# Output pairs of a hybrid decoder layer: sums of y and differences of the weights move from GpSimd to the vector engine, and the slots of the output stage are laid out anew

## The chip, the cores and the metric

The kernel is one program on one core of a Trainium2 chip. The metric is the device time of one execution in microseconds (us), as the median of several runs. The engines are called as the profile calls them: PE (TensorE matmul) with PEld (its weight load), DVE (VectorE), ACT (ScalarE), POOL (GpSimd) and SP (SyncE, which only issues DMAs). Each engine works through its own queue of instructions in order; they wait for one another by semaphores.

## The reference, cut to what matters

One decoder layer over 2048 positions of width 1024, all in float32. Its last step, where most of the change lies, is a product with the output weights, a norm over the row, a gate and a residual:

```python
h = rmsnorm(x, g_pre) * (1.0 + scale[:, None, :]) + shift[:, None, :]
proj = jnp.einsum('bsd,de->bse', h, w_in)
gu, gv, gg, rq, rk, rv, rg = jnp.split(proj, PROJ_SPLITS, axis=-1)
y_gmlp = gmlp_branch(gu, gv, gg, gmlp_ln_g, gmlp_ws, gmlp_bs)
y_ret = retention_branch(rq, rk, rv, rg, positions, ret_gn_g)
y = jnp.concatenate([y_gmlp, y_ret], axis=-1)
y = rmsnorm(jnp.einsum('bsm,md->bsd', y, w_out), g_post)
return x + gate[:, None, :] * y
```

## The kernel before

**Numbers as pairs.** Each float32 operand of the large products is split into a rounded high part (cast on ACT) and a low part (subtracted on DVE), and each product is three matmuls of 128x128 by 128x512: high by high, weights' low part, activations' low part (`mm3`, L255). In `mm3` the third matmul is the one that reads the low part of its first operand, in the output stage the low part `yl` of the y block.

**Stages.** The sequence is worked in two halves of 1024 positions. In each half come the projections by token ("prv", "pqk", "pv"), and then six units (`unit`, kinds r, r, g, u, g, u) in which a block product of 2 by 2 is done with seven products instead of eight (Strassen in Winograd's form: `PRODUCTS`). The seven products need sums of blocks of activations (S1 to S4) and of weights (T1 to T4); their results pass through three banks of PSUM, X, Y and Z, and are added up on DVE. Each unit multiplies its result into y (`used`, L784): on DVE when `ON_V` names the half and the unit, else on POOL.

**The output stage.** After the units of both halves, y is multiplied with the output weights, again by seven products. A pair is two blocks of 128 rows of y; there are eight pairs in groups of `GROUPS_OUT = (2, 1, 1, 1, 1, 1, 1)`. y was written to DRAM when it was finished (`yspill`) and is loaded again as four blocks "ya" a pair (`pair_loads`); `pair_sums` makes S1 to S4 of them ("ys") and splits each operand ("yh", "yl"). The output weights come as raw blocks "or"; `osplit` (L208) forms T1 to T4 and splits them ("wh", "wl"). There are 28 such blocks (seven products by four), and they are kept for the whole stage. `out_tail` (L671) takes the results from the banks "zX", "zY", "zZ" through the partial results s1, u2, u3, g11, c22, c21, c12, squares them on ACT (with "jz" as a dump), and adds x ("xr") before the result is stored.

**The order of the work.** The kernel writes the order out by hand. A slot is one step of a product: three matmuls. `slots.at(d, f)` puts f in the engines' queues d+1 slots later, and in a group of n pairs product i of pair j starts at slot 4*(n*i + j), counted from the group's start. This gives only the order in each queue: an instruction runs as soon as its engine has come to it and its inputs and its space are there. SP's DMAs keep the order in which they are written too.

**Space.** Most tiles take one of 80 slots of 2 KB in the pool `big` (`slot`), each new tile the slot of one that is done. Beside it there is a stack of areas, opened and closed in order: in the second half "ys" (8 tiles; in it lies the first activation block A11 until the last unit's first product is done), then "yT1" (y of the gMLP groups) and "unit1". Where an area is closed and another opened in its place, the tiles of the new one wait for the last users of the old one. In the output stage before, `begin` (L1227) closes all three after the first product and opens "out", from which x and the partial results come.

Of the kernel before, what the change touches and what calls it, by code (L numbers as in the profile page):

```python
# [11 lines left out]
F32 = mybir.dt.float32  # L12
F32R = mybir.dt.float32r
BF16 = mybir.dt.bfloat16
I32 = mybir.dt.int32
AF = mybir.ActivationFunctionType
ALU = mybir.AluOpType
# [4 lines left out]
P = 128  # L22
D = 1024
# [14 lines left out]
EXTRA_PUMPS = {(0, 4): (0, 0, 0, 0, 0, 1, 1), (0, 5): (0, 0, 0, 1, 0, 1, 1), (1, 3): (0, 0, 0, 1, 0, 1, 1),  # L38
               (1, 4): (1, 1, 0, 1, 1, 1, 1), (1, 5): (1, 0, 1, 0, 1, 1, 1)}
SLOTS = 80  # L40
ON_V = ((0, 2), (1, 4), (1, 5))
TOKEN_PASSES = 4
R_WHEN = (0, 2, 5, 6, 8, 9, 10, 11, 12, 14, 15, 16)
UNITS = (("r", 0), ("r", 1), ("g", 0), ("u", 0), ("g", 1), ("u", 1))
GROUP = {"u": 0, "g": 2, "r": 6}
PRODUCTS = (("B11", "A11"), ("T2", "S2"), ("B21", "A12"), ("T3", "S3"), ("T1", "S1"), ("T4", "A22"),
            ("B22", "S4"))
BUILD = {2: ((1, "diag", 0), (8, "row", 0), (12, "diag", 1), (19, "row", 1), (20, "x", 0), (21, "x", 1)),
# [52 lines left out]
def tile_hybrid_layer(ctx: ExitStack, tc, x, xt, wm, wg, win, wun, wout, wst, cols, rows, pos, cst,  # L101
# [40 lines left out]
    def slot(name, shape=(512,), dtype=F32, pool=None):  # L142
        return (pool or big).tile([P, *shape], dtype, name=name, tag="s")
# [9 lines left out]
    def closed(n=1):  # L153
        for _ in range(n):
            areas.pop()
            opens.pop().__exit__(None, None, None)
# [38 lines left out]
    def split(i, r, eng, gap):  # L195
        hi, lo = slot("wh", dtype=F32R), slot("wl", dtype=F32R)
        blocks[i] = (hi, lo)
        S.copy(hi, r)  # L198

        def rest():  # L200
            eng.tensor_tensor(lo, r, hi.bitcast(F32), ALU.subtract)  # L201

        if gap:
            slots.at(gap - 1, rest)
        else:
            rest()

    kept = {}  # L208

    def osplit(i, n, eng, gap):  # L210
        r, (p, kb) = raw.pop(i), divmod(n, 4)
        what = PRODUCTS[p][0]
        if what == "T2":
            t3, t2, t1 = kept["T3", kb], kept["T2", kb], kept["T1", kb] = r["B12"], r["B11"], r["B22"]
            V.tensor_tensor(t3, t1, t3, ALU.subtract)
            V.tensor_tensor(t2, t3, t2, ALU.add)
            slots.at(1, lambda: split(i, t2, eng, gap))
        elif what == "T1":
            t = kept.pop((what, kb))
            G.tensor_tensor(t, t, kept["T2", kb], ALU.subtract)  # L220
            slots.at(3, lambda: split(i, t, eng, gap))
        elif what == "T4":
            t = r["B21"]
            G.tensor_tensor(t, t, kept.pop(("T2", kb)), ALU.subtract)
            slots.at(3, lambda: split(i, t, eng, gap))
        else:
            split(i, kept.pop((what, kb)) if what == "T3" else r[what], eng, gap)

# [377 lines left out]
    ydram = ctx.enter_context(tc.tile_pool(name="ydram", bufs=1, space=bass.MemoryType.DRAM))  # L606
    yd = {}

    def yspill(half, part, cols, queue=SP):
        for q in range(2):  # L610
            if (half, part, q) not in yd:
                yd[half, part, q] = ydram.tile([P, QUAD, 4, P], F32, name=f"yd{half}{part}{q}")
            for n in cols:
                queue.dma_start(yd[half, part, q][:, :, n, :], (yR, yT)[part][half, q][n])


    def pair_loads(half, ch):
        a = {}

        def load():  # L620
            for m in range(2):
                for part in range(2):
                    t = a[f"A{m + 1}{part + 1}"] = slot("ya", (4, P))
                    SP.dma_start(t, yd[half, part, m][:, ch, :, :])

        return a, load

    def pair_sums(a, ops, size, j):

        def op(out, x, y, how):  # L630
            def run():
                if out not in a:
                    a[out] = slot("ys", (4, P))
                G.tensor_tensor(a[out], a[x], a[y], how)  # L634
                if out == "S3":
                    a.pop("A21")
            return run

        def part(key):
            def run():  # L640
                hi, lo = ops[key] = slot("yh", (4, P), F32R), slot("yl", (4, P), F32R)
                src = a[key]
                S.copy(hi, src)  # L643
                slots.at(0, lambda: V.tensor_tensor(lo, src, hi.bitcast(F32), ALU.subtract))  # L644
            return run

        def need(n):
            return 4 * (size * n + j)

        n = [need(i) for i in range(len(PRODUCTS))]  # L650
        return ((n[0] - 8, op("S1", "A21", "A22", ALU.add)), (n[0] - 6, part("A11")),
                (n[1] - 9, op("S2", "S1", "A11", ALU.subtract)), (n[1] - 6, part("S2")),
                (n[3] - 12, op("S3", "A11", "A21", ALU.subtract)), (n[2] - 6, part("A12")),
                (n[3] - 6, part("S3")), (n[6] - 17, op("S4", "A12", "S2", ALU.subtract)),
                (n[4] - 6, part("S1")), (n[5] - 6, part("A22")), (n[6] - 6, part("S4")))
# [15 lines left out]
    def out_tail(half, ch, ops, psum):  # L671
        last = (half, ch) == (1, QUAD - 1)
        ps, tmp, xr = {}, {}, []
        row = [half * HALF + (ch + QUAD * m) * P for m in range(2)]
        ss = small.tile([P, 2, 2], F32, name="zss", bufs=4)
        rs = small.tile([P, 2], F32, name="zrs", bufs=4)
        pools = []

        def temp(name):
            t = tmp[name] = pools[0].tile([P, 512], F32, name=name, tag="k", bufs=10)  # L680
            return t

        def product(n, k):
            a, bank, first = ops[PRODUCTS[n][1]], "XYXYZYZ"[n], n in (0, 1, 4)
            if first and k == 0:
                ps[bank] = psum[0].tile([P, 512], F32, name=f"z{bank}", tag=psum[1])
            mm3(ps[bank], (a[0][:, k, :], a[1][:, k, :]), blocks[OUT_BLOCKS + 4 * n + k],
                first and k == 0, k == 3, not first)

        def square(z, m, n):  # L690
            jk = pools[0].tile([P, 512], BF16, name="jz", tag="j", bufs=2)
            S.activation(jk, z, AF.Square, scale=1.0 / 32.0, accum_out=ss[:, m, n:n + 1])

        def add(dst, bank, other):
            V.tensor_tensor(temp(dst), ps[bank], tmp[other], ALU.add)

        def root(m):
            r = rs[:, m:m + 1]
            G.tensor_scalar(r, ss[:, m, 0:1], ss[:, m, 1:2], EPS, ALU.add, ALU.add)
            G.tensor_tensor(r, r, nhalf[:, 0:1], ALU.pow)  # L700

        def cols(n):
            return slice(n * 512, (n + 1) * 512)

        def gain(dst, z, n):
            V.tensor_tensor(dst, z, gg[:, cols(n)], ALU.mult)

        def result(m, n, zg):
            V.scalar_tensor_tensor(xr[m][:, cols(n)], zg, rs[:, m:m + 1], xr[m][:, cols(n)], ALU.mult,
                                   ALU.add)  # L710
            SP.dma_start(out[row[m]:row[m] + P, cols(n)], xr[m][:, cols(n)])

        def block(name, bank, other, m, n):
            return ((0, lambda: add(name, bank, other)), (1, lambda: square(tmp[name], m, n)),
                    (2, lambda: gain(tmp[name], tmp[name], n)))

        def after(n, begin):
            if n == 0:
                pools.append(begin())
                temp("s1")  # L720
                for m in range(2):
                    xr.append(pools[0].tile([P, D], F32, name="xr", tag="x", bufs=4))
                    SP.dma_start(xr[m], x[row[m]:row[m] + P, :])
            steps = (
                ((0, lambda: S.copy(tmp["s1"], ps["X"])),),
                ((0, lambda: add("u2", "Y", "s1")),),
                ((0, lambda: square(ps["X"], 0, 0)), (1, lambda: gain(temp("g11"), ps["X"], 0))),
                ((0, lambda: add("u3", "Y", "s1")),),
                block("c22", "Z", "u3", 1, 1),
                block("c21", "Y", "s1", 1, 0) + ((3, lambda: root(1)),  # L730
                                                 (8 - 4 * last, lambda: result(1, 0, tmp["c21"])),
                                                 (9 - 4 * last, lambda: result(1, 1, tmp["c22"]))),
                block("c12", "Z", "u2", 0, 1) + ((3, lambda: root(0)),
                                                 (10, lambda: result(0, 0, tmp["g11"])),
                                                 (11, lambda: result(0, 1, tmp["c12"]))))
            for t, fn in steps[n]:
                slots.at(t, fn)

        return product, after
# [481 lines left out]
                prepare(groups[0], len(PRODUCTS) * 4)  # L1221
            unit(half, un, up)

    slots.at(3, partial(yspill, 1, 1, (2, 3), S))
    pools = []

    def begin():  # L1227
        if not pools:
            closed(3)
            pools.append(opened("out"))  # L1230
        return pools[0]

# [2 lines left out]
            prepare(groups[n + 1], len(PRODUCTS) * 4 * len(group))  # L1235
        out_pairs(begin, [g[:3] for g in group])
    slots.flush()
    closed()


# [60 lines left out]
```

## Time and profile before

| what | us |
|---|---|
| median of 3 runs | 889.39 (888.69 to 890.38) |
| the profiled execution | 890.16 |
| its span in the trace | 888.4 |
| PE busy | 849.4 (96% of the span) |
| DVE busy | 670.8 (76%) |
| POOL busy | 386.3 (43%) |
| ACT busy | 311.2 (35%) |

The span runs from the first instruction to the end of the last; the profiled execution's time has 1.8 us beside it. The shares are means over stages that differ: a stage is read from its own rows.

### The profile page before, as it was taken

The page shows a single profiled execution, that of the slowest core. Times are in us where ns is not written, and L with a number is a line of the kernel's source. Part 1 is how long each engine was busy: PE and PEld are TensorE (multiplying, and loading weights), DVE is VectorE, ACT ScalarE, POOL GpSimd, SP SyncE. Part 2 cuts the span into 40 slices and gives each one's busy share as a digit, 9 for nine tenths or more (in the row PEclk, how much of TensorE's full clock was granted, in tenths as well). Part 3 has the DMA queues.
Part 4 walks back from the last instruction along what each step waited for, and adds up shares of the span by engine and source line. Part 5 has one row for each costly group of instructions (what it writes and reads, how often), then busy time and mean ns, then how long its engine had stood idle before and what let it go on. Part 6 is the DMA issues. An engine that isn't in the chain of part 4 may idle for free.

```text
span 888.4 us, 11862 instructions
## 1 busy us (share of the span) xinstructions
PE 849.4 (96%) x4074; PEld 699.1 (79%) x4074; DVE 670.8 (76%) x1255; ACT 311.2 (35%) x611; POOL 386.3 (43%) x423
## 2 busy tenths in 40 slices
PE   2999999999999999999999999999999988999996
PEld 1778888888888788888888888888888766788884
DVE  4989875666994768997786664996369887977775
ACT  4673223232363434421121121364334424333331
POOL 2041354345756446200433333784556163554551
PEclk9999999999999999999999999999999988999999
DMA  8971331210013424744122100012406742465442
GB/s 323 327 259 35 95 108 64 91 36 1 1 60 107 135 63 148 227 141 157 56 84 69 39 1 1 1 48 77 157 17 194 257 165 85 128 229 164 143 150 88
DMA packets 61884, 100.59 MB, mean 113 GB/s; under 512 B 5888, under 2 KB 22400, under 8 KB 61824
## 3 DMA queue, kind: packets, MB, share of 16 engines
q1 hardware_dynamic: 59712, 98.78, 34.0%
q10 hardware_dynamic: 2112, 1.05, 0.4%
q8 instruction: 32, 0.52, 0.2%
q14 instruction: 28, 0.23, 0.1%
HBM read 83.03 MB, written 16.78 MB: 112 GB/s over the span
## 4 chain that ended last, share of the span: by engine, by line
PE 83%; DVE 6%; DMA 4%; issue 3%; ACT 2%; POOL 1%; SPq 0%; ACTq 0%; DVEq 0%; POOLq 0%
PE pqk L258 6%; PE pqk L256 6%; PE pqk L257 6%; PE pY L256 4%; PE pY L258 3%; PE pY L257 3%; PE pv L258 3%; PE pv L256 3%; PE pv L257 3%; PE prv L257 2%; PE prv L256 2%; PE prv L258 2%; PE pX L258 2%; PE pX L257 2%; PE pX L256 2%
## 5 line engine op out<-in xcount | busy, mean ns | idle before, releaser
L256 PE MATMUL pqk<-wh,hh 128*128 128x512 f32 x240 | 102.4, 427 | 0.0
L524 POOL TENSOR_TENSOR rA<-rA,rB 128x512 f32<-128x512 f32 x32 | 42.5, 1328 | 133.1 <-DVE rB L516 99.0
L258 PE MATMUL pqk<-wh,hl 128*128 128x512 f32 x240 | 94.7, 394 | 0.0
L257 PE MATMUL pqk<-wl,hh 128*128 128x512 f32 x240 | 93.9, 391 | 0.0
L538 ACT COPY qkT<-tp 128x512 f32<-128x512 f32 x32 | 18.8, 586 | 160.1 <-PE tp L529 160.1
L201 DVE TENSOR_TENSOR wl<-wr,wh 128x512 fp32r<-128x512 f32 x62 | 64.1, 1047 | 0.2
L258 PEld LDWEIGHTS pqk<-wh,hl 128*128 128x128 f32 x240 | 45.0, 188 | 10.5
L256 PE MATMUL pv<-wh,hh 128*128 128x512 f32 x128 | 52.1, 407 | 0.0
L257 PEld LDWEIGHTS pqk<-wl,hh 128*128 128x128 f32 x240 | 45.4, 189 | 6.8 <-issue 0.2
L256 PEld LDWEIGHTS pqk<-wh,hh 128*128 128x128 f32 x240 | 45.4, 189 | 6.6 <-issue 0.2
L258 PE MATMUL pv<-wh,hl 128*128 128x512 f32 x128 | 50.1, 391 | 0.0
L257 PE MATMUL pv<-wl,hh 128*128 128x512 f32 x128 | 50.0, 390 | 0.0
L634 POOL TENSOR_TENSOR ys<-ya 128x512 f32<-128x512 f32 x16 | 22.3, 1396 | 59.6 <-DMA ya<-yd 37.3
L201 DVE TENSOR_TENSOR wl<-ut,wh 128x512 fp32r<-128x512 f32 x48 | 42.4, 902 | 1.6 <-ACT wh L198 1.4
L514 DVE TENSOR_TENSOR rA<-pqk,cos_t 128x512 f32<-128x512 f32 x28 | 19.2, 687 | 32.0 <-PE pqk L258 32.0
L258 PE MATMUL zY<-wh,yl 128*128 128x512 f32 x96 | 38.7, 404 | 2.7 <-DVE yl L644 2.7
L582 DVE TENSOR_SCALAR yq<-o,gmv,grs 128x128 f32<-128x128 f32 x64 | 23.3, 406 | 23.8 <-POOL grs L575 23.8
L256 PE MATMUL zY<-wh,yh 128*128 128x512 f32 x96 | 38.9, 405 | 2.4 <-ACT yh L643 1.3
L461 ACT ACTIVATE vh<-pv,nbv,rsv 128x128 f32<-128x128 f32 x64 | 24.1, 457 | 47.4 <-POOL nbv L456 47.4
L241 POOL TENSOR_TENSOR ut<-ur,ut 128x512 f32<-128x512 f32 x24 | 36.2, 1508 | 9.8 <-DVE yT L791 7.6
L791 POOL TENSOR_TENSOR yT<-yT,c 128x512 f32<-128x512 f32 x15 | 24.7, 1651 | 35.7 <-DVE c L811 25.9
L198 ACT CAST wh<-ut 128x512 fp32r<-128x512 f32 x48 | 28.7, 620 | 32.7 <-POOL ut L241 32.7
(253 smaller groups left out, 2594.9 us busy)
## 6 DMA issues: line engine op xcount, KB each, us to landing
wr<-in_win SPq DMA_DIRECT2D x64, 256.0 KB, 3.6
ur<-in_wun SPq DMA_DIRECT2D x48, 256.0 KB, 3.6
slab<-in_wm SPq DMA_DIRECT2D x16, 512.0 KB, 6.6
ya<-yd SPq DMA_DIRECT2D x32, 256.0 KB, 5.2
xr<-in_x SPq DMA_DIRECT2D x16, 512.0 KB, 3.8
out<-xr SPq DMA_DIRECT2D x32, 256.0 KB, 2.1
or<-in_wout SPq DMA_DIRECT2D x28, 256.0 KB, 3.5
xt<-in_xt SPq DMA_DIRECT2D x24, 256.0 KB, 4.1
```

The costliest lines, as they stand in the source:

```text
L198: S.copy(hi, r)
L201: eng.tensor_tensor(lo, r, hi.bitcast(F32), ALU.subtract)
L241: G.tensor_tensor(r[name], r[a], r[b], ALU.subtract)
L256: T.matmul(ps, l[0], r[0], start=first, stop=False, skip_group_check=reopened)
L257: T.matmul(ps, l[0], r[1], start=False, stop=False, skip_group_check=reopened)
L258: T.matmul(ps, l[1], r[0], start=False, stop=last, skip_group_check=reopened)
L461: S.activation(vh[:, g, :], ps[:, g * P:(g + 1) * P], AF.Identity, bias=nb[:, g:g + 1], scale=rs[:, g:g + 1])
L514: V.tensor_tensor(A, ps.rearrange("p (g d) -> p g d", g=8), tab["cos"][:, ch, :].unsqueeze(1).broadcast_to([P, 8, 64]), ALU.mult)
L524: G.tensor_tensor(A, A, box["B"].rearrange("p g h d -> p (g h d)"), ALU.add)
L582: V.tensor_scalar(yq[h][:, ch % QUAD, :], box["o"][:, i, :], mv[:, i, 0:1], rs[:, i:i + 1], ALU.subtract, ALU.mult)
L634: G.tensor_tensor(a[out], a[x], a[y], how)
L791: eng.tensor_tensor(y, y, by, ALU.mult)
```

## The change

S1 to S4 of the first group (the one with two pairs) and the differences T1 and T4 of the output weights are made on DVE instead of POOL, with the split of T1 and T4 two slots earlier. The loads of ya go to the area "ys" instead of a slot of `big`; in turn the partial results and jz take slots of `big`. The areas yT1 and unit1 are closed after the fifth product instead of the first, "ys" stays open, and x is loaded there, after the fifth product of each pair. The last spill of y (four DMAs) goes from ACT's queue at slot 4 of the output stage to SP's at slot 21. In the first half, unit 1 is added to `ON_V`, so that its four products into y go to DVE, and the row factors of the second half (`diag`, `row`) and two loads of x are put two to four slots later in unit 2.

```diff
-ON_V = ((0, 2), (1, 4), (1, 5))
+ON_V = ((0, 1), (0, 2), (1, 4), (1, 5))
...
-BUILD = {2: ((1, "diag", 0), (8, "row", 0), (12, "diag", 1), (19, "row", 1), (20, "x", 0), (21, "x", 1)),
+BUILD = {2: ((4, "diag", 0), (12, "row", 0), (13, "diag", 1), (21, "row", 1), (22, "x", 0), (23, "x", 1)),
...
         elif what == "T1":
             t = kept.pop((what, kb))
-            G.tensor_tensor(t, t, kept["T2", kb], ALU.subtract)
-            slots.at(3, lambda: split(i, t, eng, gap))
+            V.tensor_tensor(t, t, kept["T2", kb], ALU.subtract)
+            slots.at(1, lambda: split(i, t, eng, gap))
         elif what == "T4":
             t = r["B21"]
-            G.tensor_tensor(t, t, kept.pop(("T2", kb)), ALU.subtract)
-            slots.at(3, lambda: split(i, t, eng, gap))
+            V.tensor_tensor(t, t, kept.pop(("T2", kb)), ALU.subtract)
+            slots.at(1, lambda: split(i, t, eng, gap))
...
-    def yspill(half, part, cols, queue=SP):
+    def yspill(half, part, cols):
...
-                queue.dma_start(yd[half, part, q][:, :, n, :], (yR, yT)[part][half, q][n])
+                SP.dma_start(yd[half, part, q][:, :, n, :], (yR, yT)[part][half, q][n])
...
-                    t = a[f"A{m + 1}{part + 1}"] = slot("ya", (4, P))
+                    t = a[f"A{m + 1}{part + 1}"] = slot("ya", (4, P), pool=areas[0])
...
-                G.tensor_tensor(a[out], a[x], a[y], how)
+                (V if size > 1 else G).tensor_tensor(a[out], a[x], a[y], how)
...
-        pools = []
-
         def temp(name):
-            t = tmp[name] = pools[0].tile([P, 512], F32, name=name, tag="k", bufs=10)
+            t = tmp[name] = slot(name)
             return t
...
-            jk = pools[0].tile([P, 512], BF16, name="jz", tag="j", bufs=2)
+            jk = slot("jz", dtype=BF16)
...
         def after(n, begin):
             if n == 0:
-                pools.append(begin())
                 temp("s1")
+            if n == 4:
                 for m in range(2):
-                    xr.append(pools[0].tile([P, D], F32, name="xr", tag="x", bufs=4))
+                    xr.append(begin().tile([P, D], F32, name="xr", tag="x", bufs=4))
                     SP.dma_start(xr[m], x[row[m]:row[m] + P, :])
...
-    slots.at(3, partial(yspill, 1, 1, (2, 3), S))
+    slots.at(20, partial(yspill, 1, 1, (2, 3)))
     pools = []
 
     def begin():
         if not pools:
-            closed(3)
+            closed(2)
             pools.append(opened("out"))
         return pools[0]
...
-    closed()
+    closed(2)
```

## Rows read from the trace of the kernel before

**Rows 1.** The page: busy time, share of the span and instructions of each engine.
```profile
PE 849.4 (96%) x4074; PEld 699.1 (79%) x4074; DVE 670.8 (76%) x1255; ACT 311.2 (35%) x611; POOL 386.3 (43%) x423
```
**Rows 2.** Waits of PE: us in total, times, longest us.
```profile
PE zX L258 <- DVE yl L644: 4.3, 3, 3.7
...
PE zY L258 <- DVE yl L644: 2.7, 1, 2.7
PE zY L256 <- ACT yh L643: 1.3, 1, 1.3
PE rb_ps L325 <- DVE dgr L303: 1.2, 1, 1.2
```
**Rows 3.** By stretch, busy us of PE, PEld, DVE, ACT, POOL; clock; DMA share, GB/s.
```profile
710.44:762.87 52.43, 44.43 (x170) 34.96 (x168) 42.56 (x49) 18.27 (x39) 26.99 (x20) 0.87 0.32 106
716.95:723.78 6.83, 5.74 (x14) 4.49 (x15) 5.19 (x6) 1.78 (x4) 3.85 (x3) 0.50 0.39 120
737.43:744.26 6.83, 5.34 (x13) 4.19 (x14) 6.83 (x9) 3.29 (x8) 2.50 (x2) 0.50 0.15 41
762.87:784.26 21.39, 19.92 (x85) 15.53 (x84) 18.17 (x24) 7.57 (x18) 10.42 (x9) 1.00 0.73 240
803.60:860.72 57.12, 57.12 (x253) 47.30 (x252) 42.90 (x61) 21.16 (x48) 27.77 (x25) 1.00 0.50 166
```
**Rows 4.** Timeline of PE: start, us, line, tiles, idle before and its releaser.
```profile
718.04 0.80 PE L258 MATMUL zX<-wh,yl 128*128 128x512 f32 x1 [3.72 <-DVE yl L644]
...
738.92 0.80 PE L258 MATMUL zY<-wh,yl 128*128 128x512 f32 x1 [2.72 <-DVE yl L644]
```
**Rows 5.** Timeline of DVE in the output stage.
```profile
705.84 0.68 DVE L811 TENSOR_TENSOR c<-pZ,u 128x512 f32<-128x512 f32 x1
...
712.87 3.45 DVE L201 TENSOR_TENSOR wl<-or,wh 128x512 fp32r<-128x512 f32 x2
716.24 1.75 DVE L644 TENSOR_TENSOR yl<-ya,yh 128x512 fp32r<-128x512 f32 x1
...
743.49 0.68 DVE L706 TENSOR_TENSOR g<-zX,gg 128x512 f32<-128x512 f32 x1
744.09 0.68 DVE L644 TENSOR_TENSOR yl<-ys,yh 128x512 fp32r<-128x512 f32 x1
```
**Rows 6.** Timeline of POOL in the output stage.
```profile
703.26 1.29 POOL L634 TENSOR_TENSOR ys<-ya 128x512 f32<-128x512 f32 x1 [22.22 <-PE pZ L258]
...
710.66 3.44 POOL L220 TENSOR_TENSOR or<-or 128x512 f32<-128x512 f32 x2
...
715.73 3.39 POOL L220 TENSOR_TENSOR or<-or 128x512 f32<-128x512 f32 x2
...
732.43 2.52 POOL L224 TENSOR_TENSOR or<-or 128x512 f32<-128x512 f32 x2 [4.03 <-DMA or<-in_wout]
```
**Rows 7.** Timeline of ACT and its queue there.
```profile
710.74 11.16 ACTq L614 DMA_DIRECT2D yd<-yT  x4
722.00 0.62 ACT L198 CAST wh<-or 128x512 fp32r<-128x512 f32 x1 [10.64 <-DVE yl L644]
...
733.75 1.14 ACT L198 CAST wh<-or 128x512 fp32r<-128x512 f32 x2 [6.01 <-POOL or L224]
```
**Rows 8.** Timeline of SP's queue there: time from first issue to last.
```profile
706.94 13.12 SPq L723 DMA_DIRECT2D xr<-in_x  x2
...
727.55 3.06 SPq L190 DMA_DIRECT2D or<-in_wout  x6
```
**Rows 9.** DMA issues by line: KB each, median us to landing.
```profile
xr<-in_x SPq DMA_DIRECT2D x16, 512.0 KB, 3.8
```
**Rows 10.** Timeline of DVE and of POOL in the first half's unit 2.
```profile
292.92 1.77 DVE L303 TENSOR_TENSOR dgr<-cst_t,rsh 128x512 fp32r<-128x512 f32 x1
...
291.00 1.44 POOL L791 TENSOR_TENSOR yR<-yR,c 128x512 f32<-128x512 f32 x1 [0.53 <-ACT c L799]
```
**Rows 11.** Busy us by stretch as in rows 3, of the first half's unit 1.
```profile
272.00:292.00 20.00, 20.00 (x90) 16.57 (x89) 9.63 (x16) 7.19 (x13) 11.65 (x9) 1.00 0.37 110
```

## The prediction

> **What bounds the kernel now.** I read the page first: PE is busy for 96% of the span [rows 1], so only what PE loses in waits or to its clock can be won. The waits of PE come next: behind the load of the first inputs, which the change leaves alone, the long ones stand in the output stage, on DVE's low parts "yl" (4.3 and 2.7 us) and ACT's high part "yh" (1.3), and one of 1.2 us on the row factors "dgr" in the first half [rows 2]. Then the stretches, cut at the first zX matmul of each group. Three single pairs, 252 matmuls, take 57.12 us, or 0.2267 a matmul at full clock; so a slot is 0.68 us and a pair 19.04. The first group, 168 matmuls, should take 38.08 and takes 52.43: it loses 14.35 us. The second group takes 21.39 and loses 2.35 [rows 3].
>
> Where do the 14.35 go? About 8 are the waits above. The clock gives most of the rest: it stands at half (1.2 instead of 2.4 GHz) in two stretches of 6.83 us [rows 3], each around a wait: PE stood still for 3.72 us until 718.04, and for 2.72 until 738.92 [rows 4]. Of the first stretch 718.04 - 716.95 = 1.09 us is idle anyway, so half of the other 5.74 is lost, 2.9; of the second, in the same way, 2.7. A halving thus costs some 2.8 us.
>
> Why are the operands late? Three queues answer.
> - DVE: a subtraction of 128x512 takes 0.68 us and the next starts 0.60 after it; while POOL works, two take 3.45 and one 1.75 [rows 5]. POOL runs its T1 differences in just that time, two in 3.44 and two in 3.39 [rows 6]. One overlapped instruction costs DVE 1.75 - 0.68 = 1.07 us more.
> - ACT: the spill of y holds its queue for 11.16 us, because it waits for DVE's last product into y; the casts behind it come 10.64 us late [rows 7].
> - SP: x for the first pairs waits in the space of yT1 until that is free; from 706.94 the two issues take 13.12 us, and six loads of weights behind them start at 727.55 [rows 8]. So POOL's T4 waits 4.03 for a load [rows 6], and ACT 6.01 for T4 [rows 7].
>
> **Part by part: spill and x.** The spill in SP's queue at slot 21 stands behind all weight loads, the last of which is written at slot 18; ACT loses nothing to it any more. DVE's last product into y is long done by then, at full pace in front of slot 10, so SP does not wait there for long. What is queued behind it: x of the first pair (written behind slot 35), the next loads of ya (slot 36), x of the second (behind slot 39). x lands in 3.8 us [rows 9], 5.6 slots, and is first needed 12 slots after it is written. In single pairs SP comes to x after the stores of the pair before (slot 11) and has until slot 32. I cost this at nothing; the cover is those 12 slots, and without it a result, not PE, would be late.
>
> **ya and the partial results.** A11 of the last unit leaves "ys" after the first product of that unit, in front of the slot at which ya is loaded, so the loads need not wait. With that `big` has eight slots more where it is fullest. The partial results take slots later: counted in the code, 28 weight blocks hold 56 of 80, two pairs hold at most s1, u2, g11 and c22 each (8), one jz, 6 operand parts and 2 sums: 73. Nothing, as long as this count holds.
>
> **Sums and differences on DVE.** They are 16 instructions. The trace has no such run on DVE; the nearest rows are its subtractions, between 0.60 (back to back) and 0.68 (each alone). I count in queue order from c22 of the last unit, which starts at 705.84 [rows 5], to the low part of the first pair's S3 at slot 19. There are 28 old instructions (three additions and three products of the unit, 13 low parts of weights, 7 yl, 2 u2) and 14 new ones (S1, S2, S3 twice, T1 and T4 four times), 42. The slot count starts at 710.44, and PE reads a yl with the third matmul, 0.45 us into its slot. At 0.60 the n-th ends at 705.84 + 0.60 (n - 1) + 0.68:
> - A11 of the second pair, 12th, ends at 713.1; needed at slot 4, 713.6: in time.
> - S2, 18th, 716.7 against slot 8, 716.3: 0.4 late. S2 of the second pair, 24th, 720.3 against slot 12, 719.05: 1.3.
> - A12 of the second pair, 36th, 727.5 against slot 20, 724.5: 3.0.
> - S3, 42nd, 731.1 against slot 24, 727.2: 3.9 late, and the most; the 46th (S3 of the second pair) is 3.6 late, and then few instructions remain per slot and DVE catches up.
>
> So PE loses 3.9 us in bits of at most 1.5, where it lost 14.35. At 0.68 apiece the same walk gives 7.2. POOL is silent meanwhile, so the 1.07 a piece is gone. I take 4.8: nearer the back-to-back row, since the queue is never empty, with one in four alone because it waits for a cast. The gain is 14.35 - 4.8 = 9.5 us. The clock should hold: no single wait comes near those at which it fell, 3.72 and 2.72 [rows 4].
>
> The Trainium skill (SBUF — State Buffer, section "Who interferes with whom") says that a vector instruction with two SBUF inputs and a GpSimd one that reads SBUF exclude each other for the whole instruction. By that, a POOL difference of 1.72 would hold DVE for 1.72, not 1.07, and the 16 moved would give DVE 18 us back (estimate, 16 x (1.72 - 0.60)); by the row it is 7.5. The row agrees in kind and shows less; the sum above uses neither.
>
> **Unit 1 on DVE, row factors later.** In unit 1 DVE is busy for 9.63 of 20 us [rows 11], so four products of 0.68, or 1.75 with POOL beside them, hide in its idle time: nothing. PE's 1.2 us [rows 2] come from "dgr", which takes 1.77 beside POOL, itself behind a product into yR [rows 10]. With that gone and PE's row four slots later against three for the factors, the wait should go: between 0 and 1.2 us, I take 1.2, since one more slot is 0.68 and POOL's 1.44 is away. The x loads come two slots (1.4 us) later, with seven slots to their first use.
>
> **The second group** keeps its 2.35: its POOL sums stay where they were.
>
> The sum: 9.5 + 1.2 = 10.7 us. The profiled execution is at 890.16 (span 888.4), 0.8 above the median of 889.4; against it 879.5, against the median 878.7.
>
> **The rivals.**
> 1. Forecast, DVE slightly late: 878.7, 876 to 882 with lags of 3.9 to 7.2 and the 1.2 in doubt. Chance 0.63.
> 2. DVE is never late, because without SP's and ACT's blocks c22 itself comes earlier: 889.4 - 14.35 - 1.2 = 873.8. For it: the walk's start, 705.84, is that of the old queues. Against: 14 instructions in 17 us. 0.13.
> 3. DVE is the bound, each at 0.68, and the clock falls once: loss 7.2 + 2.8 = 10.0, gain 4.35 + 1.2, time 883.9. Against: waits of 1.5 at most. 0.13.
> 4. The wait only moves, no gain: the T4 differences now stand in DVE's queue, and if the third still finds its load at 732.4 [rows 6] it stops DVE from 725.0 (33rd in the walk) on, 7.4 us. Lag 3.9 + 7.4 and two halvings of 2.8 make 16.9, 2.5 more than before, less the 1.2: 890.7. It needs SP's loads to stay late, and x was what held them [rows 8]. 0.05. The Trainium skill (Perfetto Trace Analysis, section "Optimizing Scalar/DVE Operations") warns that moving work between these two engines might not help since they share a read port; in this kernel that would be this case.
> 5. Slower: `big` runs out. POOL's first S1 waited until PE's pZ gave a slot back, at 703.26 [rows 6], so slots are short. If the live tiles pass 80 in the output stage, a partial result on DVE waits for a product to end, up to 2.72 us (four slots), with all low parts queued behind it, once a pair: 8 x 2.72 = 21.8, less 10.7, time 900.5. It decides from eight tiles above my count of 73. 0.06.
>
> A measurement of this kernel tells about 0.2% (1.8 us) from no change. Cases 1 to 3 are faster (0.89), 4 is within it (0.04, and 0.01 of it just slower), 5 is slower: 0.07 in all. The range, 873.5 to 885, holds cases 1 to 3.
>
> **What would show it.** Right: POOL without work on "or" and on the first group's "ys", DVE's low parts at 0.68 there, ACT without its 10 us, SP's loads done by 715, clock 1.00 through the first group, and that group at 42 to 45 us; no wait on dgr. Wrong: a clock of 0.50 in it, DVE waiting for "or" or for a slot, a group above 48 us, or new waits of PE in single pairs.

## The result, and the profile after

The changed kernel takes 881.78 us (median of 4 runs, 880.52 to 882.85), the kernel before 889.3 in the same comparison. The ratio is 0.9914 with a 95% interval of 0.9896 to 0.9931: faster by 7.5 us, or 0.9%, where 10.7 were forecast (878.7); the time lies inside the range of 873.5 to 885. The profiled execution took 881.76, its span 880.0, which is 8.4 less than before; the balance below is made of spans.

The windows of the kernel after, cut at the first zX matmul of each group as in [rows 3] and with the same columns; the third line is a stretch inside the second:

```profile
708.90:752.10 43.20, 40.05 (x169) 30.99 (x168) 38.80 (x62) 19.27 (x39) 5.75 (x6) 1.00 0.48 159
752.10:776.29 24.19, 21.46 (x85) 16.70 (x84) 20.11 (x27) 8.19 (x19) 11.28 (x10) 0.93 0.66 217
764.52:767.93 3.41, 3.41 (x10) 2.67 (x9) 2.87 (x5) 0.00 (x0) 0.00 (x0) 0.50 1.03 377
776.29:795.33 19.04, 19.04 (x85) 15.77 (x84) 15.63 (x21) 7.07 (x16) 9.80 (x9) 1.00 0.57 165
```

| part of the span | before | after | change | forecast |
|---|---|---|---|---|
| up to the first group's start | 710.44 | 708.90 | -1.5 | -1.2 |
| first group | 52.43 | 43.20 | -9.2 | -9.5 |
| second group | 21.39 | 24.19 | +2.8 | 0 |
| third group | 19.34 | 19.04 | -0.3 | 0 |
| the rest | 84.8 | 84.7 | -0.1 | 0 |

The first group loses 5.12 us against its 38.08, where it lost 14.35, and its clock holds at 1.00. DVE does 13 more instructions in it (62 against 49) in 3.8 us less of busy time (38.80 against 42.56). The second group, which was to stay as it was, loses 5.15 instead of 2.35, and now has the only halved clock outside the end of the program.

The waits of PE after (us in total, times, longest), which answer to [rows 2]:

```profile
PE zX L258 <- DVE yl L644: 2.3, 4, 1.2
PE zY L256 <- DVE u L694: 2.2, 1, 2.2
PE zY L258 <- DVE yl L644: 1.2, 2, 0.6
```

The wait on "dgr" is gone. The long waits on "yl" have become five short ones in the first group, 3.15 us in all. A wait costs more than its row lists; here is the shortest of the five:

```profile
711.84 0.39 PE L257 MATMUL zX<-wl,yh 128*128 128x512 f32 x1
712.50 0.50 PE L258 MATMUL zX<-wh,yl 128*128 128x512 f32 x1 [0.27 <-DVE yl L644]
712.83 0.39 PE L256 MATMUL zX<-wh,yh 128*128 128x512 f32 x1
```

The starts lie 0.66 and 0.33 us apart, where 0.227 each is the pace: 0.53 is lost at a wait listed as 0.27. Each of the five loses some 0.27 beyond its row, which makes 4.5 of the 5.12.

In the list of waits one row is new: "u", the partial result u2 of the second group, for which PE waits 2.2 us. Its place in PE's timeline, with the longest of the five short waits above it:

```profile
726.92 0.50 PE L258 MATMUL zX<-wh,yl 128*128 128x512 f32 x1 [1.16 <-DVE yl L644]
...
763.72 0.47 PE L256 MATMUL zY<-wh,yh 128*128 128x512 f32 x1 [2.17 <-DVE u L694]
```

Where was DVE before that "u"? DVE's timeline after, and under it POOL's for the same stretch:

```profile
758.26 0.68 DVE L644 TENSOR_TENSOR yl<-ya,yh 128x512 fp32r<-128x512 f32 x1
758.86 0.74 DVE L708 SCALAR_TENSOR_TENSOR xr<-g,zrs,xr 128x512 f32<-128x512 f32 x1
759.52 1.77 DVE L708 SCALAR_TENSOR_TENSOR xr<-c,zrs,xr 128x512 f32<-128x512 f32 x1
761.22 1.75 DVE L644 TENSOR_TENSOR yl<-ys,yh 128x512 fp32r<-128x512 f32 x1
762.89 0.68 DVE L694 TENSOR_TENSOR u<-zY,s 128x512 f32<-128x512 f32 x1
```

```profile
759.33 1.42 POOL L634 TENSOR_TENSOR ys<-ya,ys 128x512 f32<-128x512 f32 x1
760.71 1.72 POOL L634 TENSOR_TENSOR ys<-ya 128x512 f32<-128x512 f32 x1
763.11 1.27 POOL L634 TENSOR_TENSOR ys<-ys,ya 128x512 f32<-128x512 f32 x1 [0.68 <-POOL ys L634]
```

In these rows DVE is never idle in front of "u"; it is late because two of its instructions took 1.77 and 1.75 us while POOL made sums. POOL's row at 759.33 is S4 of the second group, which was there before too. The one at 760.71 is S1 of the *third* group. The timeline of POOL before has that sum 20 us later, waiting for its block to be loaded; the low part in front of "u" then took 0.68, and PE's wait was half as long. Here are the rows of POOL, DVE and PE before:

```profile
780.76 1.64 POOL L634 TENSOR_TENSOR ys<-ya 128x512 f32<-128x512 f32 x1 [9.38 <-DMA ya<-yd]
```

```profile
771.85 0.68 DVE L644 TENSOR_TENSOR yl<-ys,yh 128x512 fp32r<-128x512 f32 x1
772.45 0.68 DVE L695 TENSOR_TENSOR u<-zY,s 128x512 f32<-128x512 f32 x1
```

```profile
773.28 0.47 PE L256 MATMUL zY<-wh,yh 128*128 128x512 f32 x1 [1.06 <-DVE u L695]
```

SP's queue after says why the sum can come so early (start, time from first issue to last); the last row is that of the third group's loads before:

```profile
701.22 13.57 SPq L614 DMA_DIRECT2D yd<-yT  x4
714.88 0.58 SPq L190 DMA_DIRECT2D or<-in_wout  x1
...
723.93 0.80 SPq L624 DMA_DIRECT2D ya<-yd  x2
...
728.10 0.33 SPq L624 DMA_DIRECT2D ya<-yd  x1
728.48 0.42 SPq L190 DMA_DIRECT2D or<-in_wout  x1
728.95 13.25 SPq L624 DMA_DIRECT2D ya<-yd  x5
```

```profile
772.82 1.87 SPq L624 DMA_DIRECT2D ya<-yd  x4
```

With these eight loads of "ya" after, the second and the third group's blocks are all issued by 742, ahead of the first stores of results (752.19). Before, the third group's four stood behind six of those stores and were issued from 772.82. The first two rows show a second thing that was not forecast: the spill stood in SP's queue ahead of the last weight loads and held it for 13.57 us.

### The profile page after: what moved, and what is told of

It reads as the page before. It is cut to its first block, busy times and chain, and to the rows that moved or that the text cites. A ratio compares the mean times of both kernels' runs of the same rounds, so it can differ in the third digit from the quotient of the medians.

```text
span 880.0 us, 11841 instructions
## 1 busy us (share of the span) xinstructions
PE 845.7 (96%) x4074; PEld 696.3 (79%) x4074; DVE 673.3 (77%) x1275; ACT 313.0 (36%) x611; POOL 358.1 (41%) x403
## 4 chain that ended last, share of the span: by engine, by line
PE 84%; DVE 6%; issue 3%; DMA 3%; ACT 2%; POOL 1%; SPq 0%; DVEq 0%; POOLq 0%; ACTq 0%
PE pqk L258 6%; PE pqk L256 6%; PE pqk L257 6%; PE pY L258 4%; PE pY L256 4%; PE pY L257 3%; PE pv L256 3%; PE pv L258 3%; PE pv L257 3%; PE prv L257 3%; PE prv L256 2%; PE pX L256 2%; PE prv L258 2%; PE pX L258 2%; PE pX L257 2%
## 5 line engine op out<-in xcount | busy, mean ns | idle before, releaser
L698 POOL TENSOR_SCALAR zrs<-zss 128x1 f32<-128x1 f32 x16 | 18.2, 1140 | 128.7 <-ACT jz L691 128.0
```

## The experiments

The theory after the result: DVE's queue sets the first group, much as the prediction walked it, and the lost 2.8 us of the second group come from the third group's sums, which POOL now makes beside DVE's low part in front of u2. Rivals: the gain comes from what was taken out of SP's and ACT's queues and not from DVE; the loss comes from something else in the new space, or from the spill in SP's queue. Three sets of four kernels ran, each set with runs of the kernel before beside it (889.14, 890.32 and 889.92). Medians of different sets are compared by their ratio to before; 95% intervals stand in brackets.

**dve_only**: the kernel before, with only the sums of the first group and T1, T4 on DVE.

```diff
-            G.tensor_tensor(t, t, kept["T2", kb], ALU.subtract)
-            slots.at(3, lambda: split(i, t, eng, gap))
+            V.tensor_tensor(t, t, kept["T2", kb], ALU.subtract)
+            slots.at(1, lambda: split(i, t, eng, gap))
...
-                G.tensor_tensor(a[out], a[x], a[y], how)
+                (V if size > 1 else G).tensor_tensor(a[out], a[x], a[y], how)
```

> The kernel before with S1 to S4 of the first group and T1, T4 on DVE, and nothing else of the change. Theory of three queues (POOL's collisions with DVE, ACT held by the spill, SP held by x, each enough for a late operand): x still holds SP and the loads of the weights for T4 come at 725 to 732 us as before, now in front of DVE's queue, so the first group loses 9 to 15 us of its 52.4 instead of the change's 5.1, and the time is 883 to 889. Rival, the collisions alone made the wait: the first group loses 5 to 6 as with the whole change, and the time is 879 to 881 (no 1.2 from unit 1, no 2.8 lost in the second group).

Measured: 884.92, 0.9956 [0.9939, 0.9974]. The first group takes 47.15 and loses 9.07, at the low end of what was expected; one long wait remains in it, and the clock is halved for 3.41 us behind it. PE's timeline, then DVE's:

```profile
731.93 0.69 PE L258 MATMUL zX<-wh,yl 128*128 128x512 f32 x1 [4.80 <-DVE yl L644]
```

```profile
729.37 0.69 DVE L224 TENSOR_TENSOR or<-or 128x512 f32<-128x512 f32 x1 [3.51 <-DMA or<-in_wout]
```

DVE's T4 waits for a load of weights that SP issued behind x, and the low part stands behind T4 in DVE's queue. That is the prediction's fourth case, with 3.51 us instead of 7.4. The second group is as before (21.41). So DVE's part alone is worth 5.3 us in the first group, and leaves one long wait standing.

**space_only**: the changed kernel, with the sums, T1, T4 and the first half put back; only the space, the spill and x differ from before.

```diff
-                (V if size > 1 else G).tensor_tensor(a[out], a[x], a[y], how)
+                G.tensor_tensor(a[out], a[x], a[y], how)
...
-ON_V = ((0, 1), (0, 2), (1, 4), (1, 5))
+ON_V = ((0, 2), (1, 4), (1, 5))
```

(T1, T4 and `BUILD` go back in the same way.)

> The change without anything moved to DVE and without the edits of the first half: only the loads of ya in the area ys, partial results in slots, the areas closed and x loaded after the fifth product, the spill in SP's queue. Theory of three queues: the wait of 3.7 us on the second pair's yl, which the collisions made, stays with its half clock (2.9), the waits at S3 go or shrink; the first group loses 6 to 10 us and the time is 882 to 886. Rival, ACT and SP alone made the waits: the first group loses 5 or less, time 881 or less. Rival, the collisions alone: 14 us lost as before, 888 to 890.

Measured: 888.07, 0.9989 [0.9976, 1.0002]: no gain that can be told, where the theory had 882 to 886. The rival with 888 to 890 hits the time, but not by its reason (14 us lost as before). The first group loses 10.55 instead of 14.35, yet the second takes 22.35, 1.0 more than before, with PE's new wait already there:

```profile
770.92 0.47 PE L256 MATMUL zY<-wh,yh 128*128 128x512 f32 x1 [2.17 <-DVE u L694]
```

The two halves add up: 5.3 and 3.8 us make 9.1 in the first group, and the whole change gains 9.2 there. The collision belongs to the space half: dve_only doesn't have it, space_only does. SP's queue isn't emptied in that half: the spill holds it for 19.57 us in space_only.

**no_unit1**: the changed kernel with `ON_V` and `BUILD` of before.

```diff
-ON_V = ((0, 1), (0, 2), (1, 4), (1, 5))
+ON_V = ((0, 2), (1, 4), (1, 5))
```

> The change without its two edits of the first half (unit 1 on DVE, row factors later). If those gave the 1.2 us: PE's wait on dgr comes back with 1.0 to 1.3 us, all of the output stage as in the changed kernel but 1.2 us later, time 882.5 to 883.5. Rival, the row factors had time anyway once POOL's work elsewhere moved: no wait on dgr, time as the changed kernel, 881.8.

Measured: 882.79, 0.9935 [0.9915, 0.9954]. PE's wait on "dgr" is back with 1.17 us; the term of 1.2 was right. The first group starts 2.6 us later than after, not 1.2 as expected: the rest follows a wait of 0.74 us on DVE's "c" in the last unit (at 708.61), which all_v has too (0.67) and the kernels before and after haven't.

**all_v**: the sums of all groups on DVE.

```diff
-                (V if size > 1 else G).tensor_tensor(a[out], a[x], a[y], how)
+                V.tensor_tensor(a[out], a[x], a[y], how)
```

> The change with S1 to S4 of all groups on DVE, none on POOL. The second group takes 24.2 us with the change and 21.4 before: theory, ya of the third group is loaded earlier, so that POOL's sums of it run at 760.7 beside DVE's low parts (1.75 us instead of 0.68) and make u2 late by 1.1, PE waits 2.2 and the clock falls for 3.4 us. Then with no sums on POOL the wait on u2 is under 1.0, the clock stays at 1.00 and the second group takes 20 to 21.5: 878 to 879.5 in all. Rival, DVE is simply behind with the results of two pairs: five more instructions in front of u2 make it 2 to 3 us later still, the second group takes 25 to 27, time 883 to 885.

Measured: 879.23, 0.9888 [0.9871, 0.9905]; the wait on "u" is 0.54 us, at full clock, as the theory had it. **third_v** asks the same of two instructions alone: only S1 and S2 of the third group go to DVE (a flag `third` is set for it).

```diff
-                (V if size > 1 else G).tensor_tensor(a[out], a[x], a[y], how)
+                (V if size > 1 or third and out in ("S1", "S2") else G).tensor_tensor(a[out], a[x], a[y], how)
```

> The changed kernel with S1 and S2 of the third group alone on DVE, behind u2 of the second group; nothing else. Theory: POOL's early S1 of the third group, beside DVE's last low part in front of u2, is what the change added to the second group. Then that low part takes 0.68 instead of 1.75, PE's wait on u2 falls from 2.2 to 0.9 to 1.2, and the second group takes 21 to 22 (24.2 with the change, 21.4 before): 878.5 to 880. Rival, something else makes u2 late (the longer DVE queue, slots): wait 2.2 and 24 as with the change.

Measured: 880.24, 0.9890 [0.9875, 0.9904], 0.2 above the range of the theory. DVE's timeline of third_v, then PE's:

```profile
760.84 1.77 DVE L708 SCALAR_TENSOR_TENSOR xr<-c,zrs,xr 128x512 f32<-128x512 f32 x1
762.53 0.68 DVE L644 TENSOR_TENSOR yl<-ys,yh 128x512 fp32r<-128x512 f32 x1
763.13 0.68 DVE L694 TENSOR_TENSOR u<-zY,s 128x512 f32<-128x512 f32 x1
```

```profile
763.96 0.47 PE L256 MATMUL zY<-wh,yh 128*128 128x512 f32 x1 [1.09 <-DVE u L694]
```

The low part in front of "u" is back at 0.68, the wait falls from 2.17 to 1.09, and the second group takes 21.58 at full clock. That is the rise of 2.8 us but for 0.2, from two instructions. The ratios' intervals of all_v and third_v still overlap that of the changed kernel; what tells them apart is the second group in the traces: 24.19 after, 21.58 in third_v, 20.57 in all_v.

**spill_act** puts the spill back into ACT's queue at slot 4; **x_early** loads x after the first product again.

```diff
-    slots.at(20, partial(yspill, 1, 1, (2, 3)))
+    slots.at(3, partial(yspill, 1, 1, (2, 3), S))
```

> The changed kernel with the last spill back in ACT's queue at slot 4. In the kernel before it held ACT for 11.2 us. Theory now: it did so because DVE's last product into y was late; with that product at 713.6 ACT comes to the spill when it is done, loses 2 to 3 us for the four issues, SP is freed of 13.6 us of waiting for it, and the first group loses 4.5 to 6: time 881 to 883. Rival, the spill holds ACT for 8 us or more whatever DVE does: casts late, first group loses 9 or more, 885 to 887.

```diff
-            if n == 4:
+            if n == 0:
```

> The changed kernel with yT1 and unit1 closed, and x loaded, after the first product as before. Theory: the loads of x wait in SP's queue for the end of the spill, the weight loads for T4 and B22 behind them come 5 to 12 us later, and since T4 now stands in DVE's queue, DVE stops for them: first group loses 8 to 14, time 884 to 889. Rival, where x is loaded does not matter once the spill has left ACT: 881 to 883.

Measured, spill_act: 880.73, 0.9902 [0.9879, 0.9924]. The spill holds ACT's queue for 2.67 us, where it held it for 11.16 [rows 7], since DVE's product is no longer late. The first group (42.92) is no worse. Moving the spill was worth nothing once DVE was on time. Measured, x_early: 882.45, 0.9921 [0.9905, 0.9938]; the first group loses 7.31, 2.2 more than after, and less than the 8 to 14 expected. The time is in the rival's range and can't be told from the changed kernel's: in the profiled execution the second group keeps full clock and takes 1.5 less (22.69). DVE's timeline shows T4 waiting for a load behind x, as the prediction's fourth case had it, but for 2.48 us and not 7.4:

```profile
723.41 0.69 DVE L224 TENSOR_TENSOR or<-or 128x512 f32<-128x512 f32 x1 [2.48 <-DMA or<-in_wout]
```

In both the third group's S1 still runs beside DVE's low part (at 760.25 and 762.94) and the wait on "u" is 2.17. So neither the spill's place nor x's brings the loads of "ya" forward. Of the space half there remains that "ya" lies in "ys" and the partial results in slots; these two were not tried apart.

**t_pool** puts T1 and T4 back on POOL, **s_pool** the sums of the first group.

```diff
-            V.tensor_tensor(t, t, kept["T2", kb], ALU.subtract)
-            slots.at(1, lambda: split(i, t, eng, gap))
+            G.tensor_tensor(t, t, kept["T2", kb], ALU.subtract)
+            slots.at(3, lambda: split(i, t, eng, gap))
```

> The changed kernel with T1 and T4 back on POOL as before; S1 to S4 of the first group stay on DVE. By the collisions (1.07 us for each POOL instruction that meets one of DVE, against 0.60 for the same instruction on DVE) DVE is 0 to 4 us slower up to S3: first group loses 5 to 9, time 882 to 886. Rival, DVE's own count of instructions is the only bound: eight fewer, first group loses 0 to 2, time 877 to 879.

```diff
-                (V if size > 1 else G).tensor_tensor(a[out], a[x], a[y], how)
+                G.tensor_tensor(a[out], a[x], a[y], how)
```

> The changed kernel with S1 to S4 of the first group back on POOL; T1 and T4 stay on DVE. By the collisions alone, six of eight in the stretch: first group loses 5 to 8. S2 and S3 then also go through POOL (1.3 to 1.7 us) to ACT and back to DVE, and may be late by themselves. Time 882 to 886. Rival as in the run with T1 and T4 on POOL: fewer instructions, less lost, 878 to 880.

Measured: t_pool 883.04, 0.9919 [0.9903, 0.9934]; s_pool 883.46, 0.9924 [0.9906, 0.9941]. Each part is worth little beside the other. In t_pool the first group is even shorter (40.21: it loses 2.1, not the 5 to 9 expected), but it starts 4.2 us later, so that the expected time came for another reason. POOL makes T1 in the last unit, and beside it a sum of DVE takes 1.67 us and a low part of the weights 1.21. PE's wait on "u" there is 2.53 us, where the kernel after waits 0.94 (at 697.89), and the clock is halved behind it:

```profile
700.50 0.50 PE L256 MATMUL pY<-sh,wh 128*128 128x512 f32 x1 [2.53 <-DVE u L810]
```

In s_pool the first group loses 8.0, at the upper end of what was expected, with waits of 2.33 and 1.56 at its start, where POOL's sums run beside DVE's low parts.

**slow_pump**: the low parts of the output weights, which DVE makes ahead of their use, come every fourth slot of the first group instead of every second. **all_v_slow_pump** has this and all_v. **late_results** has both, and six of the eight final results of the first group (`result`, 0.75 us each on DVE) come 12 slots later.

```diff
-                    if done[0] < len(worder) and k % size == 0:
+                    if done[0] < len(worder) and k % (2 * size) == 0:
```

> The changed kernel, but the 12 output weight blocks left for the first group are split one every fourth slot instead of every second. Theory: the 5.1 us that the first group still loses are DVE's order, 42 subtractions and sums in front of the first pair's S3, in which T1, T4 and their low parts stand earlier than PE needs them. Then some ten of them move behind the yl parts, the first group loses 0 to 2 us, and the time is 3 to 5 less than the change: 877 to 879. Rival, the yl parts are late for their own chain (sum on DVE, cast on ACT, subtraction) or for loads: still 4 to 5 lost, 881 to 882.5.

> Sums of all groups on DVE, and the weights split every fourth slot. Both theories right: the first group loses 0 to 2, the second at most 1.5, no half clock in the output stage: 874.5 to 876.5. If the weights' low parts then come too late for the later products, or the second group's DVE work grows by what was put off, it is no better than the sums of all groups on DVE alone: 879.

```diff
-                                                 (8 - 4 * last, lambda: result(1, 0, tmp["c21"])),
-                                                 (9 - 4 * last, lambda: result(1, 1, tmp["c22"]))),
+                                                 (8 - 4 * last + late[0], lambda: result(1, 0, tmp["c21"])),
+                                                 (9 - 4 * last + late[0], lambda: result(1, 1, tmp["c22"]))),
```

(`late` is 0 and 12 for the first pair, 12 and 12 for the second; the results of the other row take `late[1]`.)

> Sums of all groups on DVE and the weights split every fourth slot, and six of the eight results of the first group's pairs put 12 slots later, behind u2 of the second group. Theory: what the second group still loses (3.4 us of 22.4) is DVE's order again, the results standing in front of u2 and g11's wait. Then it takes 19.5 to 20.5, and the time is 874 to 875.5. Rival, the loss is from elsewhere (s1 on ACT, slots): 22 and 876.7 as without it.

Measured: 879.27, 0.9888 [0.9870, 0.9906]; 876.73, 0.9855 [0.9839, 0.9871]; 875.48, 0.9837 [0.9822, 0.9852]. The windows of slow_pump, then those of late_results, first and second group of each:

```profile
708.54:747.51 38.97, 38.66 (x170) 31.37 (x168) 37.16 (x60) 19.01 (x39) 4.18 (x4) 1.00 0.54 176
747.51:773.54 26.03, 22.37 (x86) 16.47 (x85) 21.88 (x28) 8.18 (x19) 12.87 (x12) 0.93 0.62 202
```

```profile
709.12:748.00 38.88, 38.71 (x170) 31.38 (x168) 37.07 (x61) 19.04 (x39) 3.25 (x3) 1.00 0.53 176
748.00:768.91 20.91, 20.20 (x85) 15.46 (x84) 19.05 (x31) 6.99 (x17) 5.44 (x6) 1.00 0.58 189
```

With fewer low parts in between, the first group loses 0.9 us instead of 5.1, as the theory had it: what was left there was the length of DVE's queue. The time of 879.27 still lies just above its range of 877 to 879, for in slow_pump 1.8 of this comes back as loss in the second group: that group starts 4.6 us earlier than after, but DVE, with the first group's results in its queue and POOL's sums beside it, comes to "u" only 2.8 us earlier (760.12 against 762.89). With the sums off POOL (all_v_slow_pump) the second group loses 3.4, where at most 1.5 was expected; with the results later as well it loses 1.9, again a little more than expected, and 0.6 of the 1.5 gained comes back in the third group (19.65). The times of these two can't be told apart. The last version is some 6.8 us faster than the changed kernel by the ratios, whose intervals are apart.

## Why the prediction was right in the first group and short of the time

- **First group, 9.5: right, 9.2.** Counted in the trace, the low part of S3 is the 41st instruction from c22 on, one fewer than in the walk, as S1 of the first pair comes ahead of c22 (at 704.28). c22 starts at 704.88 and that low part at 729.78, which makes 24.90 / 40 = 0.62 apiece, the pace behind the 4.8; it ends at 730.47, 4.8 behind slot 24, as taken. A little luck is in it: the missing instruction gave 0.6 back, and c22 starts 4.0 us ahead of the first group, not 4.6. The blocks of the list are late; A11 of the second pair (a wait of 0.27), which the walk had in time, and A12 of the first (0.56) are late as well. The longest wait is 1.16, where 1.5 was the bound. The clock holds, as forecast.
- **Which part does it.** The prediction named three queues and put the gain on DVE's. By the runs DVE's part alone gives 5.3 of it, and the space half (space, spill and x) 3.8.
- **The spill, at nothing: the cost was right, the reason wrong.** It was to stand behind all weight loads; the row at 701.22 shows it ahead of the last ones. The loads of x for the first pairs, written behind slot 35, stand between those loads too, from 715.51 on. So SP's DMAs are not issued in the order of the slots, which the description of the kernel and the prediction took for granted, and an argument from slot numbers doesn't hold for them. The kernel says so itself: the engines whose order it fixes by hand (`ORDERED`, L19) are PE, DVE, ACT and POOL, and SP isn't among them. SP is held for 13.57 us by DVE's last product. DVE then waits 0.49 us for one load (its T4 at 721.36), which is one of the prediction's own signs of being wrong, but a small one. "SP's loads done by 715" fails for the same reason: the last is issued at 728.48.
- **x, ya and slots.** x behind the fifth product is worth 2.2 us in the first group (x_early). From c22 to the low part of S3 DVE waits once, for the load (0.49), never for a slot, and the single pairs run at 19.04: the fifth case didn't come.
- **Unit 1, 1.2: right** (1.18 of wait gone, back in no_unit1).
- **"The second group keeps its 2.35: its POOL sums stay where they were": the step that failed, by 2.8 us.** The second group's sums did stay. The third group's did not: the prediction cost the new home of "ya" by asking whether its loads must wait, and didn't ask what they start when they come earlier. S1 of the third group moved from 780.76 to 760.71, beside the low part in front of u2. That adds 1.1 to PE's wait. In the profiled execution the clock then stands at half for 3.41 us, of which half is lost, 1.7. Together 2.8. The prediction took the clock to fall only at waits near 2.72 and 3.72; here it fell after one of 2.17.

With this term the sum is 10.7 - 2.8 = 7.9; the spans differ by 8.4, the medians by 7.5.

## What to carry to other kernels

Where an edit gives a load its space earlier, follow what that load releases, on every engine, up to the next group: work that used to wait for data is work that was kept out of the way. Where two engines slow each other, look for the instruction that stands ahead of the bound engine's next wait, and move the other engine's work from beside it; here two instructions were worth 2.6 us of a group, 1.1 of it as a wait and the rest mostly by the clock. An operand made ahead of its use in a full queue is a delay of everything behind it: spreading such work over twice the slots took 4.2 us out of the group, though 1.8 of them came back in the next.

## What the runs showed of the hardware

**DVE and POOL take turns.** The prediction read 1.75 for 0.68 as a slowing of 1.07. The ends of the rows say more. POOL's sum of 759.33 ends at 760.75 and DVE's 759.52 at 761.29; POOL's 760.71 ends at 762.43 and DVE's 761.22 at 762.97: each time DVE ends 0.55 us later (0.54 in the rounded rows). So do all 24 of DVE's instructions with both inputs in SBUF that start during one of POOL's sums in the output stage after. The four that start there with one input from PSUM ("u<-zY,s") keep their 0.68; here is one of them, then POOL's sum:

```profile
782.63 0.68 DVE L694 TENSOR_TENSOR u<-zY,s 128x512 f32<-128x512 f32 x1
```

```profile
782.24 1.63 POOL L634 TENSOR_TENSOR ys<-ya 128x512 f32<-128x512 f32 x1
```

An instruction of DVE with two inputs in SBUF thus waits out what is left of POOL's, and then takes its time. The Trainium skill (SBUF — State Buffer, section "Who interferes with whom") has it so: such a pair contends for a shared read interface, by an exclusive lock, and a vector instruction with at most one SBUF input, outside the two-port modes, does not contend. The trace agrees, with 24 of 24 and 4 of 4, where the prediction said that it showed less; the price is what remains of the other's instruction, up to 1.1 here, and not the whole 1.72 that the prediction drew from the page.

The other rule of the Trainium skill that the prediction named (Perfetto Trace Analysis, section "Optimizing Scalar/DVE Operations"), that moving work between the two might not help, did not come true here: dve_only is such a move alone and gains 0.44% [0.26, 0.61].

**The clock after the same wait.** PE's wait of 2.17 us on "u" is followed by a halved clock in the profiled executions of after, spill_act, no_unit1 and t_pool (and one of 2.15 in slow_pump), and by none in those of space_only, s_pool and x_early. Nor does the length of a wait decide it alone: in the first group of space_only the clock is halved behind a wait of 3.42 us and stays full behind one of 3.08, and in that of x_early it stays full behind one of 2.57. Of the four runs of after, one has a mean clock of 0.998 and 880.52 us, the others 0.995 or 0.996 and 881.76 to 882.85. What decides it stays open; 1.7 us of the failed term hang on it.
